# Two MLPs in a written order, with their norms turned by token halves

## The chip, the cores and the metric

One core of a Trainium2 chip runs the whole program. It has a matrix engine (TensorE, PE; its weight loads are listed apart as PEld), a vector engine (VectorE, DVE), an activation engine (ScalarE, ACT), a general engine (GpSimd, POOL) and a queue that issues the DMAs (SyncE, SP). Each works through its own list of instructions in order and waits on semaphores for the others. The metric is the time of one execution on the device in microseconds, smaller being better.

## The reference

Two residual layers over 512 tokens of 1024 features, all in fp32. Layer 0 mixes tokens by latent attention (MLA), layer 1 by an mLSTM; each mixer is followed by the same kind of MLP:

```python
def sqrelu_mlp(h, w1, w2):                       # w1 1024 x 4096, w2 4096 x 1024
    return jnp.square(jax.nn.relu(h @ w1)) @ w2

for i in range(2):                               # mixer 0: MLA, mixer 1: mLSTM
    x = x + mixer(rms_norm(x, norm_mix[i]))
    x = x + sqrelu_mlp(rms_norm(x, norm_ffn[i]), ffn_w1[i], ffn_w2[i])
```

`rms_norm` divides each token's row by the root of its mean square and multiplies by a gain per feature.

## The kernel before

The program has four stages in a row: MLA, MLP 0, mLSTM, MLP 1. x lies in SBUF with tokens on the partitions, as eight tiles `xs[t, f]` of 128 tokens by 512 features.

Every fp32 product is made of three matmuls in a rounded format: each operand is split into a high part (a cast) and a low part (operand less high part), and `mm3` (L174 to L176) adds high x high, high x low and low x high. So each weight tile of 128 x 1024 that arrives by DMA (`wr` for w1 and the mixers, `tw` for w2) costs a cast on ACT (`wh`, L160) and a subtraction on DVE (`wl`, L164).

A stage ends with `out_proj`: eight matmul groups that add to x on DVE (L700), and then the next stage's norm. The norm squares x on ACT (L251, the row sums fall out of it), turns x on PE with 128 x 128 transposes (`turn`, L238), and splits what comes out of PSUM into high (`xg`, ACT, L255) and low part (`xg`, DVE, L256), with the gain. The factor 1/rms per token is applied later: in an MLP to what is added to x, in the mixers by rows or columns. `rows_sb` (L198, L200, L232) spreads the factors along a row for mLSTM.

An MLP (`ffn`) has 32 "first" products, F0 to F31: each takes 128 of the 4096 hidden features, 8 x 3 matmuls of 512 columns (all tokens), then relu and square on ACT into `z` (L735, L737). Four of them make a chunk. The second product works by chunks of 512 hidden features. Tokens, hidden and output features are halved, and the 2 x 2 block product is made of seven products (`product`, L766) and not of eight: the price is four sums of z (L743 to L746, 256 columns each) and four sums of w2 (t1 to t4, L761 to L764, 1024 columns) on POOL. The blocks of w2 are called b11, b12, b21, b22. The seven z operands are split by a cast on ACT (`hh`, L748) and a subtraction on DVE (`hl`, L749), in pieces of 768 and 1024 columns. A product, P(c, 0) to P(c, 6), is 12 matmuls of 512 columns, and its result is added to x on DVE with the token's factor (`x<-tp,r,x`, L784).

The order: MLA is written out engine by engine, and its instructions are pinned to program order by the wrappers `ipe`, `idve`, `iact` and `ipool`. Everything after it, so `out_proj`, both MLPs and the mLSTM, is ordered by the scheduler that builds the program; the code gives it six F ahead (`lead = 6`) and one F after products 0, 2, 4 and 5 of a chunk. Each engine runs the list so made in order. PSUM banks come from the pools `mm` (three banks of 512 columns), `tp` (four) and `po` (one). At the end of MLP 0 the norm of mLSTM is turned in token halves (`Norm.half`) after the last two products; MLP 1 turns x itself (`out`, L806, L808) and stores it by DMA.

## Time and profile before

| what | value |
|---|---|
| median of 3 runs | 1155.81 us (1153.32 to 1156.1) |
| the profiled execution, its own time | 1154.43 us |
| its span | 1152.6 us |
| mean granted clock of TensorE | 0.991 |
| PE, DVE, ACT, POOL busy | 97%, 72%, 49%, 39% |

The span runs from the first to the last instruction of the profile. A row of the timeline gives the start, the busy time, engine, line, operation, output and inputs by the program's names, and in square brackets how long the engine stood idle before it and what it waited for. A matmul's busy time overlaps the next one's, so the pace of matmuls is read from their starts. The chain of work that ended last is 87% PE.

### The profile page before, as it was taken

How to read it: one execution, taken by the hardware profiler on the slowest of the kernel's cores; microseconds unless marked ns; L12 is line 12 of the kernel's file. 1: busy time of each engine (PE TensorE's matmuls, PEld its weight loads, DVE VectorE, ACT ScalarE, POOL GpSimd, SP SyncE). 2: the span in 40 equal slices, each digit the busy share in tenths (PEclk: the TensorE clock that was granted, in tenths of full speed). 3: DMA queues.
4: the chain of work that ended last, by engine and by line, in shares of the span. 5: the costliest groups of instructions: out<-in, count | busy, mean ns of one | idle time of the engine just before them, and what ended most of it. 6: DMA issues, size and time to landing. Idle time of an engine off the chain costs nothing.

```text
span 1152.6 us, 15433 instructions
## 1 busy us (share of the span) xinstructions
PE 1113.0 (97%) x5682; PEld 944.3 (82%) x5682; DVE 835.5 (72%) x1289; ACT 564.7 (49%) x962; POOL 451.8 (39%) x475
## 2 busy tenths in 40 slices
PE   7899999999999999999989999989999999999997
PEld 7889987878888888888778898877888888888875
DVE  7689997446788788778966465534477788788787
ACT  4578776455445444544454343333544454444542
POOL 6677785115355335434401011100265245335441
PEclk9999999999999999999989999999999999999999
DMA  6301111341432442343013222223422432442222
GB/s 205 109 24 47 38 56 40 126 163 57 128 109 63 122 128 80 103 129 92 19 58 109 73 74 73 79 57 103 146 76 89 129 110 63 121 127 82 66 73 74
DMA packets 31916, 104.27 MB, mean 90 GB/s; under 512 B 3424, under 2 KB 6240, under 8 KB 31840
## 3 DMA queue, kind: packets, MB, share of 16 engines
q1 hardware_dynamic: 31840, 103.27, 29.2%
q8 instruction: 45, 0.74, 0.3%
q14 instruction: 31, 0.25, 0.1%
HBM read 101.16 MB, written 2.10 MB: 90 GB/s over the span
## 4 chain that ended last, share of the span: by engine, by line
PE 87%; DVE 7%; issue 2%; POOL 2%; ACT 1%; DMA 1%; SPq 0%; DVEq 0%; ACTq 0%; POOLq 0%
PE mm L174 14%; PE mm L175 14%; PE mm L176 14%; PE tp L779 7%; PE tp L781 7%; PE tp L780 7%; PE tp L80 7%; PE mm L80 5%; PE tp L175 2%; PE tp L176 2%; PE tp L174 2%; DVE wl L164 2%; PE po L80 2%; DVE x L784 2%; PE mm L238 1%
## 5 line engine op out<-in xcount | busy, mean ns | idle before, releaser
L174 PE MATMUL mm<-xg,wh 128*128 128x512 f32 x640 | 251.2, 393 | 0.1
L176 PE MATMUL mm<-xg,wl 128*128 128x512 f32 x640 | 249.4, 390 | 0.0
L175 PE MATMUL mm<-xg,wh 128*128 128x512 f32 x640 | 249.2, 389 | 0.0
L164 DVE TENSOR_TENSOR wl<-wr,wh 128x1024 fp32r<-128x1024 f32 (+2 forms) x108 | 139.0, 1288 | 147.7 <-ACT wh L160 146.4
L160 ACT CAST wh<-wr 128x1024 fp32r<-128x1024 f32 (+2 forms) x108 | 111.1, 1029 | 252.7 <-PE mm L175 198.1
L164 DVE TENSOR_TENSOR wl<-tw,wh 128x1024 fp32r<-128x1024 f32 x112 | 185.6, 1658 | 49.6 <-ACT wh L160 49.6
L160 ACT CAST wh<-tw 128x1024 fp32r<-128x1024 f32 x112 | 117.8, 1055 | 122.2 <-PE mm L175 58.8
L780 PE MATMUL tp<-wl,hh 128*128 128x512 f32 x440 | 172.2, 391 | 2.3 <-DVE wl L164 2.3
L779 PE MATMUL tp<-wh,hh 128*128 128x512 f32 x440 | 170.5, 390 | 1.3 <-DVE x L784 1.3
L781 PE MATMUL tp<-wh,hl 128*128 128x512 f32 x440 | 171.4, 390 | 0.0
L784 DVE SCALAR_TENSOR_TENSOR x<-tp,r,x 128x512 f32<-128x512 f32 x220 | 158.9, 741 | 1.2 <-PE tp L781 1.2
L174 PEld LDWEIGHTS mm<-xg,wh 128*128 128x128 f32 x640 | 120.3, 188 | 25.9 <-issue 1.0
L175 PEld LDWEIGHTS mm<-xg,wh 128*128 128x128 f32 x640 | 120.3, 188 | 25.4 <-issue 1.0
L176 PEld LDWEIGHTS mm<-xg,wl 128*128 128x128 f32 x640 | 120.2, 188 | 24.9
L749 DVE TENSOR_TENSOR hl<-z,hh 128x768 fp32r<-128x768 f32 x64 | 105.2, 1644 | 12.1 <-ACT hh L748 12.1
L780 PEld LDWEIGHTS tp<-wl,hh 128*128 128x128 f32 x440 | 82.6, 188 | 21.5 <-DVE wl L164 4.5
L779 PEld LDWEIGHTS tp<-wh,hh 128*128 128x128 f32 x440 | 82.6, 188 | 19.0 <-ACT t L251 1.5
L781 PEld LDWEIGHTS tp<-wh,hl 128*128 128x128 f32 x440 | 82.6, 188 | 16.9
L743 POOL TENSOR_TENSOR z<-z 128x256 f32<-128x256 f32 x32 | 23.6, 737 | 175.3 <-ACT z L737 175.3
L748 ACT CAST hh<-z 128x768 fp32r<-128x768 f32 x64 | 60.5, 945 | 43.8 <-POOL z L746 42.8
L761 POOL TENSOR_TENSOR tw<-tw,tw 128x1024 f32<-128x1024 f32 x16 | 38.3, 2394 | 92.7 <-DMA tw<-in_w 90.1
L745 POOL TENSOR_TENSOR z<-z 128x256 f32<-128x256 f32 x32 | 25.5, 796 | 121.8 <-ACT z L737 121.8
(283 smaller groups left out, 2065.0 us busy)
## 6 DMA issues: line engine op xcount, KB each, us to landing
wr<-in_w SPq DMA_DIRECT2D x64, 512.0 KB, 3.6
tw<-in_w SPq DMA_DIRECT2D x64, 512.0 KB, 3.7
wr<-in_w_qkv SPq DMA_DIRECT2D x8, 640.0 KB, 3.9
wr<-in_w_oa SPq DMA_DIRECT2D x8, 512.0 KB, 3.6
wr<-in_w_mo SPq DMA_DIRECT2D x8, 512.0 KB, 3.6
wr<-in_w_ob SPq DMA_DIRECT2D x8, 512.0 KB, 3.6
wr<-in_w_v SPq DMA_DIRECT2D x6, 512.0 KB, 4.0
wr<-in_w_z SPq DMA_DIRECT2D x8, 336.0 KB, 4.4
```

The source lines that it names most:

```text
L80: return lambda *args, **kw: tc.keep_in_program_order(f(*args, **kw)) if self.on else f(*args, **kw)
L160: act.copy(hi[:, :n], raw[:, :n])
L164: dve.tensor_sub(lo[:, :n], raw[:, :n], hi[:, :n].bitcast(F32))
L174: pe.matmul(out, lhsT=lh, rhs=rh, start=start, stop=False)
L175: pe.matmul(out, lhsT=lh, rhs=rl, start=False, stop=False)
L176: pe.matmul(out, lhsT=ll, rhs=rh, start=False, stop=stop)
L748: nc.scalar.copy(hi[:, b], zp[:, b])
L749: nc.vector.tensor_sub(lo[:, b], zp[:, b], hi.bitcast(F32)[:, b])
L779: pe.matmul(ps, lhsT=lh, rhs=rh, start=new and p == 0, stop=False, skip_group_check=skip)
L780: pe.matmul(ps, lhsT=lh, rhs=rl, start=False, stop=False, skip_group_check=skip)
L781: pe.matmul(ps, lhsT=ll, rhs=rh, start=False, stop=p == 1, skip_group_check=skip)
L784: nc.vector.scalar_tensor_tensor(xs[k], ps, r2[:, k[0]:k[0] + 1], xs[k], op0=mult, op1=add)
```

## The change

1. `out_proj` is pinned to program order. Its last group of products goes by token blocks. After block 2 the first token half of the norm (`half(0, m)`, 16 transposes) is turned, then block 3's matmuls follow. The second half is left in `norm.tail`, and the MLP does it between its first products. F0's weight is split in `out_proj` already.
2. The MLP's first two products F0 and F1 are multiplied in two token halves each, 48 matmuls of 256 columns in place of 24 of 512.
3. All other work of the MLP is in a written order on PE, DVE, ACT and POOL: a list of units (F or P), weights split two units ahead and loaded four ahead, the z splits one or two units after the square, and the sums of w2 at fixed units, t2, t3 and t4 written over b11, b12 and t1.
4. The last chunk uses eight plain products of 12 matmuls, without sums.
5. At the end of MLP 0 the norm halves are turned between the last products, and features 4 to 7 of half 1 after the first V product of mLSTM. The factors are made by halves, and mLSTM's `rows_sb` moves behind the gates.
6. At the end of MLP 1 x is turned and stored between the last products, its last piece by single token blocks. Buffers for temporaries fall from 3 to 2, those for w2 grow from 5 to 6.

```diff
+    def out_proj(wsrc, lhs, layer, z0=None, w0=None):
+
+
+        z1 = [ps_tp() if z0 else ps_mm() for _ in range(3)] + [pp.tile([P, 512], F32, tag="po", bufs=1, name=nm("po"))]
+        todo = [(1, z1)]
+        if not z0:
+            z0 = [ps_tp() for _ in range(NB)]
+            todo.append((0, z0))
+        for j in range(3):
+            for f, z in todo:
+                w = load_w(wsrc[f, j], D)
+                for t in range(NB):
+                    for k in (2 * j, 2 * j + 1):
+                        o_mm(z[t], w, k, t, lhs, ipe)
+        last = [(z0, w0, (KD - 1,)) if w0 else (z0, load_w(wsrc[0, 3], D), (KD - 2, KD - 1)),
+                (z1, load_w(wsrc[1, 3], D), (KD - 2, KD - 1))]
+        norm = Norm(C_NF + layer * KD)
+        iact.on = True
+        for t in range(NB):
+            for z, w, ks in last:
+                for k in ks:
+                    o_mm(z[t], w, k, t, lhs, ipe)
+            for f, (z, _, _) in enumerate(last):
+                idve.tensor_add(xs[t, f], xs[t, f], z[t])
+            if t == 0:
+                norm.first = split_w(load_raw(a["w1"][layer, 0], D), D, iact, idve)
+            elif t == 2:
+                for m in range(0, KD, 2):
+                    norm.half(0, m)
+            for f in range(2):
                 norm.square(t, f)
-            for m in range(4 * f, 4 * f + 4):
-                norm.block(m)
-        return norms.append(norm)
+        norm.tail = [lambda m=m: norm.half(1, m, ps_tp) for m in range(0, KD, 2)]
+        iact.on = False
+        norms.append(norm)
 
     norms = []
...
+        def s_sum(c, n):
+
+            b = lambda n: tw[c, n]
+            if n == "t1":
+                tw[c, n] = fp.tile([P, D], F32, tag="tw", bufs=6, name=nm("tw"))
+                ipool.tensor_sub(b("t1"), b("b12"), b("b11"))
+            else:
+                x, y, to = {"t2": ("b22", "t1", "b11"), "t3": ("b22", "b12", "b12"), "t4": ("b21", "t2", "t1")}[n]
+                ipool.tensor_sub(b(to), b(x), b(y))
+                tw[c, n] = b(to)
...
+        def l_mm(th, f, t, part=slice(0, 12)):
+            ps = bank["L", f][t]
+            todo = []
+            for h in range(2):
+                wh, wl = ws["L", f"b{h + 1}{f + 1}"]
+                for p in range(2):
+                    lh, ll = (x[:, ((A11, A12), (3, A22))[th][h], t * P:(t + 1) * P] for x in hs[NC - 1, p])
+                    rh, rl = (x[:, p * 512:(p + 1) * 512] for x in (wh, wl))
+                    todo += [(lh, rh), (lh, rl), (ll, rh)]
+            for n in range(12)[part]:
+                ipe.matmul(ps, lhsT=todo[n][0], rhs=todo[n][1], start=n == 0, stop=n == 11)
...
+        units = [("F", i) for i in range(5)]
+        n = 5
+        for c in range(NC - 1):
+            for k in range(7):
+                units.append(("P", c, k))
+                if k in ((0, 2, 4, 5) if c < NC - 2 else (0, 1, 3)):
+                    units.append(("F", n))
+                    n += 1
+        at = {u: s_ for s_, u in enumerate(units)}
+
+        def ahead(s_):
+
+            if s_ + 4 < len(units) and units[s_ + 4][0] == "F":
+                f_load(units[s_ + 4][1])
+            if s_ + 2 < len(units):
+                u = units[s_ + 2]
+                if u[0] == "F":
+                    f_split(u[1])
+                else:
+                    s_split(u[1], u[2])
+                    if u[2] == 0:
+                        s_sum(u[1], "t2")
+                    elif u[2] == 1:
+                        s_sum(u[1], "t4")
+
+
+        ws["F", 0] = norm.first
+        f_load(1)
+        f_load(2)
+        ps = [ps_mm(), ps_mm()]
+        f_mm(ps[0], 0, HALVES[0])
+        for do in norm.tail[:2]:
+            do()
+        f_split(1)
+        f_mm(ps[1], 1, HALVES[0])
+        for do in norm.tail[2:]:
+            do()
+        u_ = norm.stat()
+        idve.reciprocal(r2, u_)
+        f_load(3)
+        f_split(2)
+        f_mm(ps[0], 0, HALVES[1])
+        f_post(ps[0], 0)
+        f_mm(ps[1], 1, HALVES[1])
+        f_load(4)
+        f_split(3)
+        f_post(ps[1], 1)
+        s_load(0, ("b11", "b12"))
+        s_sum(0, "t1")
+        s_load(0, ("b21", "b22"))
+        s_sum(0, "t3")
+        for s_ in range(2, len(units)):
+            u = units[s_]
+            if u[0] == "F":
+                ps = ps_mm()
+                f_mm(ps, u[1])
+                ws.pop(u)
+            else:
+                post = s_mm(u[1], u[2])
...
+            ahead(s_)
+            s_now[0] = s_
+            while later and later[0][0] <= s_:
+                later.pop(0)[1]()
+            if u[0] == "F":
+                f_post(ps, u[1])
+            else:
+                post()
+                c, k = u[1], u[2]
+                if k == 2:
+                    s_load(c + 1, ("b11", "b12"))
+                elif k == 4:
+                    s_load(c + 1, ("b21", "b22"))
+                elif k == 5 and c < NC - 2:
+                    s_sum(c + 1, "t1")
+                elif k == 6 and c < NC - 2:
+                    s_sum(c + 1, "t3")
+                if c == NC - 2 and k > 3:
+                    if k == 4:
+                        l_split("b11", False)
+                    elif k == 5:
+                        l_split("b21", False)
+                    else:
+                        l_split("b12", True)
         nxt = None if last else Norm(C_NM + KD)
-        lead, i = 6, 0
...
+        for n, (th, f) in enumerate(((0, 0), (0, 1), (1, 0), (1, 1))):
+            bank["L", f] = [ps_tp(), ps_tp()]
+            for t in range(2):
+                if last and n == 3 and t == 1:
+                    l_mm(th, f, t, slice(0, 8))
+                    out(4, (2,))
+                    l_mm(th, f, t, slice(8, 12))
+                else:
+                    l_mm(th, f, t)
+                if n == 0 and t == 0:
+                    l_split("b22", True)
+                if n == 2 and t == 0:
+                    half(0, (0, 2, 4, 6))
+                if n == 3 and t == 0:
+                    half(1, (0, 2))
+                y_add(2 * th + t, f, bank["L", f][t])
+                if not last:
+                    nxt.square(2 * th + t, f)
+        if last:
+            out(4, (3,))
+        else:
+            nxt.tail = [lambda m=m: nxt.half(1, m, ps_tp) for m in (4, 6)]
             norms.append(nxt)
+        iact.on = ipool.on = False
...
+                if h == 0 and t == 0:
+                    iact.on = True
+                    for do in norm.tail:
+                        do()
+                    iact.on = False
+                    roots(1)
                 nc.scalar.activation(vh[:, t, 0:DV], ps[:, 0:DV], AF.Copy, scale=r[:, t:t + 1])
```

*ACT at the start of MLP 0, before.* `wh` are weight casts (3456 and 3490 are those of F0 and F1), `t,ssq` squares of x, `xg` the norm's high parts.

```order
L160 CAST wh_3303<-wr_3301 128x1024
L160 CAST wh_3456<-wr_3454 128x1024
L160 CAST wh_3490<-wr_3488 128x1024
L255 ACTIVATE xg_3335<-mm_3360,cst 128x512
L255 ACTIVATE xg_3336<-mm_3367,cst 128x512
L251 ACTIVATE t_3388,ssq_3351<-x_3189 128x512
L251 ACTIVATE t_3390,ssq_3351<-x_3193 128x512
L251 ACTIVATE t_3392,ssq_3351<-x_3197 128x512
L160 CAST wh_3534<-wr_3532 128x1024
```

After the change, same place (3463 is F1's weight, and F0's was cast further up; `tp` banks hold half 1):

```order
L80 ACTIVATE xg_3298<-mm_3382,cst 128x256
L80 ACTIVATE t_3391,ssq_3307<-x_3183 128x512
L80 ACTIVATE t_3393,ssq_3307<-x_3185 128x512
L80 ACTIVATE t_3406,ssq_3307<-x_3187 128x512
L80 ACTIVATE t_3408,ssq_3307<-x_3189 128x512
L80 ACTIVATE xg_3291<-tp_3445,cst 128x256
L80 ACTIVATE xg_3292<-tp_3445,cst 128x256
L80 ACTIVATE xg_3293<-tp_3454,cst 128x256
L80 ACTIVATE xg_3294<-tp_3454,cst 128x256
L80 CAST wh_3463<-wr_3415 128x1024
```

F1's weight cast stood ahead of the first part of the norm, and now it stands behind four squares and four splits of half 1.

*ACT at the end of MLP 0, before.* Squares and splits of mLSTM's norm.

```order
L255 ACTIVATE xg_3434<-mm_5881,cst 128x256
L251 ACTIVATE t_5979,ssq_3450<-x_3197 128x512
L251 ACTIVATE t_5981,ssq_3450<-x_3201 128x512
L255 ACTIVATE xg_3435<-mm_5881,cst 128x256
L255 ACTIVATE xg_3436<-mm_5890,cst 128x256
L160 CAST wh_6191<-wr_6189 128x1024
L251 ACTIVATE t_5983,ssq_3450<-x_3195 128x512
L251 ACTIVATE t_5985,ssq_3450<-x_3199 128x512
L255 ACTIVATE xg_3437<-mm_5890,cst 128x256
```

After; 5998 and 6197 are weights of mLSTM (V and q), still placed by the scheduler:

```order
L80 ACTIVATE xg_5769<-mm_5867,cst 128x256
L80 ACTIVATE xg_5770<-mm_5867,cst 128x256
L80 ACTIVATE xg_5771<-mm_5876,cst 128x256
L80 ACTIVATE xg_5772<-mm_5876,cst 128x256
L80 ACTIVATE xg_5773<-mm_5885,cst 128x256
L160 CAST wh_5998<-wr_5996 128x1056
L80 ACTIVATE xg_5774<-mm_5885,cst 128x256
L160 CAST wh_6197<-wr_6195 128x1024
L80 ACTIVATE xg_5775<-mm_5894,cst 128x256
L80 ACTIVATE xg_5776<-mm_5894,cst 128x256
```

The squares of half 0 have moved ahead, and two casts of mLSTM weights stand between the splits of half 0.

*POOL at a chunk boundary in the middle of MLP 0, before.* `z` rows are the sums of z, `tw` rows t1 to t4.

```order
L761 TENSOR_TENSOR tw_4003<-tw_3996,tw_3995 128x1024
L762 TENSOR_TENSOR tw_4004<-tw_3998,tw_4003 128x1024
L743 TENSOR_TENSOR z_3877<-z_3877 128x256
L744 TENSOR_TENSOR z_3877<-z_3877 128x256
L746 TENSOR_TENSOR z_3877<-z_3877 128x256
L763 TENSOR_TENSOR tw_4005<-tw_3998,tw_3996 128x1024
L764 TENSOR_TENSOR tw_4006<-tw_3997,tw_4004 128x1024
```

After, with DVE's list of the same place behind it (3984 is the low part of b11, whose tile 3817 t2 is written over):

```order
L80 TENSOR_TENSOR z_3850<-z_3850 128x256 x4
L80 TENSOR_TENSOR tw_3956<-tw_3819,tw_3817 128x1024
L80 TENSOR_TENSOR tw_3817<-tw_3894,tw_3956 128x1024
L80 TENSOR_TENSOR tw_3819<-tw_3894,tw_3819 128x1024
L80 TENSOR_TENSOR tw_3956<-tw_3892,tw_3817 128x1024
```

```order
L80 TENSOR_TENSOR wl_3984<-tw_3817,wh_3983 128x1024
L80 TENSOR_TENSOR hl_3929<-z_3850,hh_3928 128x1024
L80 TENSOR_TENSOR wl_4007<-wr_3946,wh_4006 128x1024
L80 SCALAR_TENSOR_TENSOR x_3183<-tp_3710,r_740_3414,x_3183 128x512
L80 SCALAR_TENSOR_TENSOR x_3187<-tp_3711,r_740_3414,x_3187 128x512
L80 TENSOR_TENSOR wl_4030<-tw_3956,wh_4029 128x1024
```

The four sums of w2 stand in one block behind the sums of z, where before t1 and t2 went in among them.

## Rows read from the trace of the kernel before

**Rows 1.** the page's busy line of TensorE: busy us, share, instructions

```profile
PE 1113.0 (97%) x5682; PEld 944.3 (82%) x5682; DVE 835.5 (72%) x1289; ACT 564.7 (49%) x962; POOL 451.8 (39%) x475
```

**Rows 2.** stretches: length, PE, PEld, DVE, ACT, POOL busy, granted clock, DMA share, GB/s

```profile
248.50:268.50 20.00, 20.00 (x90) 16.55 (x89) 7.18 (x7) 8.38 (x12) 6.74 (x6) 1.00 0.42 144
586.00:591.00 5.00, 4.29 (x15) 2.77 (x14) 2.99 (x8) 3.51 (x8) 0.00 (x0) 0.58 0.01 3
804.00:812.00 8.00, 6.26 (x35) 4.91 (x34) 6.62 (x12) 6.81 (x13) 0.00 (x0) 0.79 0.51 186
```

**Rows 3.** timeline of PE, MLA to MLP 0: start, us, operation, [idle, releaser]

```profile
242.24 1.60 PE L238 MATMUL mm<-cst,x 128*128 128x128 f32 x12
245.71 2.11 PE L238 MATMUL mm<-cst,x 128*128 128x128 f32 x12 [1.88 <-DVE xg L256]
247.93 0.50 PE L174 MATMUL mm<-xg,wh 128*128 128x512 f32 x1
```

**Rows 4.** timeline of PE, mLSTM to MLP 1

```profile
804.23 1.60 PE L238 MATMUL mm<-cst,x 128*128 128x128 f32 x12
807.49 4.28 PE L238 MATMUL mm<-cst,x 128*128 128x128 f32 x20 [1.66 <-DVE xg L256]
812.15 0.40 PE L175 MATMUL mm<-xg,wh 128*128 128x512 f32 x1
```

**Rows 5.** timeline of PE, MLP 0 to mLSTM

```profile
544.55 0.39 PE L779 MATMUL tp<-wh,hh 128*128 128x512 f32 x1
585.61 2.05 PE L200 MATMUL tp<-t,ones 128*128 128x512 f32 x2 [0.61 <-ACT xg L255]
590.93 0.36 PE L174 MATMUL mm<-wh,xg 128*128 128x264 f32 x1 [0.71 <-DVE xg L256]
```

**Rows 6.** timeline of ACT, splits of norm halves, MLP 0 to mLSTM

```profile
585.04 0.84 ACT L255 ACTIVATE xg<-mm,cst 128x256 fp32r<-128x256 f32 x2 [0.37 <-PE mm L238]
586.18 0.86 ACT L255 ACTIVATE xg<-mm,cst 128x256 fp32r<-128x256 f32 x2 [0.31 <-DVE xg L256]
```

**Rows 7.** timeline of ACT and DVE, weight split and squares

```profile
242.71 1.03 ACT L160 CAST wh<-wr 128x1024 fp32r<-128x1024 f32 x1
244.22 0.62 ACT L251 ACTIVATE t<-x 128x512 f32<-128x512 f32 x1
244.74 0.19 ACT L251 ACTIVATION_READ_ACCUMULATOR t<-x 128x1 f32 x1
401.45 1.22 DVE L164 TENSOR_TENSOR wl<-wr,wh 128x1024 fp32r<-128x1024 f32 x1 [2.78 <-ACT wh L160]
```

**Rows 8.** timeline of POOL and DVE, a sum and a low part at once

```profile
435.99 2.40 POOL L761 TENSOR_TENSOR tw<-tw,tw 128x1024 f32<-128x1024 f32 x1
437.04 2.44 DVE L164 TENSOR_TENSOR wl<-tw,wh 128x1024 fp32r<-128x1024 f32 x1 [0.34 <-ACT wh L160]
```

**Rows 9.** timeline of DVE and POOL, residual adds, sums and low part of z

```profile
402.59 1.47 DVE L784 SCALAR_TENSOR_TENSOR x<-tp,r,x 128x512 f32<-128x512 f32 x2
403.98 1.05 DVE L749 TENSOR_TENSOR hl<-z,hh 128x768 fp32r<-128x768 f32 x1
402.65 0.74 POOL L743 TENSOR_TENSOR z<-z 128x256 f32<-128x256 f32 x1 [1.45 <-ACT z L737]
```

**Rows 10.** timeline of PE and DVE at the end

```profile
1142.87 0.39 PE L781 MATMUL tp<-wh,hl 128*128 128x512 f32 x1
1143.10 2.70 PE L238 MATMUL mm<-cst,x 128*128 128x128 f32 x20
1147.74 0.69 DVE L806 COPY t<-mm 128x512 f32<-128x512 f32 x1 [2.39 <-ACT t L808]
```

**Rows 11.** timeline of PE, cadence of 256 columns

```profile
639.92 0.28 PE L175 MATMUL mm<-wl,xg 128*128 128x256 f32 x1
640.04 0.28 PE L176 MATMUL mm<-wh,xg 128*128 128x256 f32 x1
```

**Rows 12.** timeline of PE, last head of mLSTM

```profile
757.04 0.44 PE L994 MATMUL tp<-cst,hb 128*128 128x128 f32 x2 [3.59 <-DVE hb L987]
```

More of the change, by code (lines that the diff above doesn't have):

```diff
@@ L673, in mla @@
                     o_unit(*ready[0])
[L674 removed]
+        for k, m in fill:
             o_unit(k, m)
         load_x()
[L677 removed]
+        out_proj(a["w_oa"], oT, 0, zo, wo[3])
     def o_mm(ps, w, k, t, lhs, pe=nc.tensor):
@@ L798, in out, with split @@
-        def out(th, m):
+            hs[c, p] = hi, lo
+            def split(b):
+                iact.copy(hi[:, b], z[:, b])
+                idve.tensor_sub(lo[:, b], z[:, b], hi.bitcast(F32)[:, b])
+            if plain:
+                later.append([s_now[0] + 1, lambda: split(slice(0, 4))])
+                return
+            ipool.tensor_add(z[:, S1], z[:, A21], z[:, A22])
+            ipool.tensor_sub(z[:, S2], z[:, S1], z[:, A11])
+            ipool.tensor_sub(z[:, S3], z[:, A11], z[:, A21])
@@ L800, in out @@
+        def out(m, ts):
             ps = ps_mm()
-            for n in range(2):
-                for t in range(2):
-                    turn(ps, (2 * n + t) * P, m + n, 2 * th + t)
+            nt = len(ts)
+            for n in range(4 // nt):
+                for i, t in enumerate(ts):
+                    turn(ps, (nt * n + i) * P, m + n, t)
             o = tmp()
-            if m % 4:
-                nc.vector.tensor_copy(o, ps)
-            else:
-                nc.scalar.copy(o, ps)
@@ L831, in ffn @@
-        if not last:
+            if m % 4 and nt > 1:
+                idve.tensor_copy(o, ps)
+            else:
+                iact.copy(o, ps)
+            nc.sync.dma_start(yT[m:m + 4 // nt, :, ts[0] * P:(ts[-1] + 1) * P].rearrange("m p t -> p m t"),
+                              o.rearrange("p (m t) -> p m t", t=nt * P))
+        units = [("F", i) for i in range(5)]
[6 more added lines that the diff above has]
+                    n += 1
@@ L1008, in trunk @@
         mlstm(pool)
-    with stage("ffnp1", 3) as pool:
+    with stage("ffnp1", 2) as pool:
         ffn(pool, 1, True)
```

229 lines of the change are left out of this document (95 added, 134 removed).

## The prediction, made before the result was known

> **What bounds the kernel now.** I read the page's busy shares first: TensorE (PE) is busy 97% of the span [rows 1], so a gain can only come from the few stretches in which it waits, or from fewer matmuls. Next the busy time by stretch: in 20 us of steady MLP work PE is busy for all 20.00 us with 90 matmuls, or 0.2267 us a piece after rounding over the whole MLP [rows 2]; both MLPs keep that pace from the first product to the 32nd "first" product. So nothing is to be had inside an MLP, and what can be had lies at five seams. Then the timeline of PE at each seam, which shows what it waited for.
>
> *MLA to MLP 0* [rows 3]: the last out_proj matmul gives way at 242.23, 24 transposes follow with an idle stretch of 1.88 us that ends on a VectorE (DVE) split of the normed input, and the first product starts at 247.93 (248.04 in effect, because its second matmul waits too). That is 5.8 us, of which the 24 transposes at 0.12 are 2.9: a loss of 2.9.
>
> *MLP 0 to mLSTM* [rows 5]: from the end of the 32nd first product (544.55) to the first V matmul (590.93, in effect 591.0) 46.5 us pass for 132 matmuls (29.9 us), 32 transposes (3.8) and two for the R row. The R row's matmuls take 2.05 us since the granted clock is 0.58 of full in that stretch [rows 2], so partly at 1.2 and partly at 2.4 GHz. Loss: some 12.
>
> *mLSTM to MLP 1* [rows 4]: 804.23 to 811.92 (the row at 812.15 less one matmul), 32 transposes of 0.12 = 3.8, loss 3.9, with a clock of 0.79 [rows 2].
>
> *The end* [rows 10]: the last matmul starts at 1142.87 and the last copy ends at 1148.43; the span ends 4.2 later. From the 32nd first product (1108.41) it is 44.2 us.
>
> *mLSTM's last head* [rows 12]: 3.59 us idle before the last transposes.
>
> **The change, part by part.** The profiled execution took 1154.43 us (span 1152.6); the median of the runs is 1155.81, so 1.4 is added at the end.
>
> *Twelve more matmuls per MLP* (the last chunk by eight plain products of 12 instead of seven): 12 x 0.2267 = 2.72 us each, on the path, charged below to the second and fourth seam.
>
> *Seams one and three.* Half 0 of the norm is now turned before the last token block of out_proj. Its four banks of 512 columns come from a pool of three, so the fourth waits until the splits of the first are through; those stand on DVE behind the two residual adds of block 2. Residual add and split end some 2.6 us after block 2's last matmul, three banks of transposes take 1.44: 1.2 lost. Then F0 is multiplied in its first half (24 matmuls at 0.12 [rows 11] = 2.9) and 8 transposes of half 1 follow. What is late next is the weight of F1. In the new order its cast on ScalarE (ACT) stands behind four squares and the four splits of half 1, and before the change it was done ahead of the norm. ACT's queue from block 2's end: the first bank through at 2.5, three more banks at 1.14 each [rows 6], 5.9; four squares at 0.81 [rows 7], 9.1; two banks of half 1, 11.2; the cast 1.03, 12.2; and DVE's low part 1.22 more [rows 7], 13.4. PE by then has 16 transposes (1.92), the wait (1.2), nine matmuls of block 3 (2.04), F0's half (2.87) and 8 transposes (0.96) = 9.0, and two matmuls of F1 (0.24) before it needs the low part: it stands for 13.4 - 9.24 = 4.2. F0 and F1 in halves cost 2 x 24 x (2 x 0.1197 - 0.2267) = 0.6. After a wait of that length the clock may be halved, as it is at seam three now after 1.66 idle: 8 us at 0.79 are 3.4 us at the low level, 1.7 lost. Seam one stays at full clock now after 1.88, so there it is a cost of 0 to 1.7, and I take it. Seam one: 1.2 + 4.2 + 0.6 + 1.7 = 7.7 against 2.9, **4.8 worse** (3.1 with the clock up). Seam three: there the accumulators lie in the same pool and the wait comes out at 4.0, 1.2 + 4.0 + 0.6 + 1.7 = 7.5 against 3.9, **3.6 worse** (1.9). If ACT's splits run at 0.42 apiece without waiting for DVE, F1's wait shrinks to 2; if the squares slip behind the residual adds it grows to 6.
>
> *Seam two.* The halves are turned between the last products. What remains is 29.9 us of matmuls, 24 transposes (2.9), 1.2 for the fourth bank as above, and a wait of half 1: ACT has two casts of mLSTM weights between the splits of half 0, and these need buffers that the third product still reads. After that product ACT and DVE have two casts (2.06), three splits (1.4), DVE's last split (0.47) and two residual adds (1.5), 5.4 in all, beside 2.72 of PE: 2.7 left over. 36.7 against 46.5 saves 9.8. Back go 2.72 (the plain products), 8 transposes after the first V product (0.96) and the R row, done later at full clock (0.9): **5.2 better**. Without the wait of half 1 it is 7.9, with a halved clock 3.5.
>
> *Seam four.* 29.9, 28 transposes between the matmuls (3.4), the last residual add (0.95), 4 transposes (0.5), a copy (0.6), a wait for a buffer of output (0.9, from the present one-for-one use of buffers) and the same 4.2 after it: 40.4 against 44.2, less 2.72, **1.1 better** (-1 to 2).
>
> *Last head of mLSTM.* Eight transposes wait for the slowest of the four normed blocks, and not two: **0.4 worse** (0 to 1).
>
> *The written order inside the MLPs.* The work is the same, but DVE's and GpSimd's (POOL's) can't be regrouped any more. Rows show what that may cost: a DVE subtraction of two tiles in SBUF that starts while POOL subtracts two tiles takes 2.44 us, twice its 1.22, and ends 1.05 us after POOL's 2.40 [rows 8]. A residual add with an input in PSUM takes its usual 0.74 beside POOL [rows 9]. The Trainium skill ("SBUF — State Buffer", the section on the shared port pair) says why: a DVE instruction with two SBUF inputs and a GpSimd instruction that reads SBUF hold one port pair in turn, each for the whole instruction. The trace agrees (2.44 for 1.22). By that rule the two engines' times add up where their order ties them together; if they merely slowed each other a little, the term below would be nil.
>
> At each chunk boundary the new order ties this chain: after an odd first product relu and square (1.5 with the hand-over), four sums of z on POOL at 0.74 (3.0), then by turns DVE's low part of a w2 block (1.22), the low part of z (1.05), POOL's sum t1 (2.40), the low part of b11 (1.22), which t2 must await because it is written over b11, the second part of z (1.22), t2 (2.40) and the low part of the next w1 block (1.22). That is 13.7, and 15.2 with the 1.5. PE needs the last of them after 60 matmuls and two more, 62 x 0.2267 = 14.05. One after the other it is 1.1 us late at each of 12 boundaries (six per MLP); where the first low part slips between POOL's sums while those wait, it isn't late. I take a quarter, 0.25 x 12 = **3 worse** (0 to 13), nearer nil since the same amount of work loses nothing now [rows 2].
>
> Sum: -4.8 - 3.6 + 5.2 + 1.1 - 0.4 - 3.0 = 5.5 us worse; 1154.4 + 5.5 + 1.4 = **1161.3**.
>
> **Rivals.**
> - *The seams close.* If F1's weight is split in time (it needs ACT's queue some 4 us shorter than I read it), seams one and three gain 1.1 and 2.1 and not lose 8.4, seam two gains 7.9, seam four 1.1, the last head -0.4: 11.8 better, 1144; with half of it, 1150. For it: the transposes have left the dead stretch. Against it: the place of that cast on ACT. It decides from the point at which F1 waits for less than 1 us: the change is faster.
> - *It cancels.* The clock stays up at seams one and three (3.4 back) and the boundaries lose nothing (3 back): 5.5 - 6.4 = -0.9, 1155. For it: 1.88 us idle leave the clock up now.
> - *The chain at the boundaries is fully serial.* 12 x 1.1 = 13 in place of 3: 1171. By the skill's rule of the port pair this is the outcome if nothing overlaps; the rows show the turn-taking itself, not its sum over this order.
>
> **How the numbers follow.** The forecast 0.45, the seams close 0.21, it cancels 0.21, serial boundaries 0.13. What three runs can tell from no change is about 0.3%, 3.5 us: 1152.3 to 1159.3. The forecast and the serial case are slower, though a part of the forecast's own spread (clock, quarter of the chain) ends inside the 3.5; the closing seams are faster but for a small part. Slower 0.51, same 0.25, faster 0.24. The range goes from the half-closed seams, 1149, to the serial boundaries, 1172; the forecast's own is 1157 to 1166.
>
> **What would show it.** In the changed profile: (1) PE idle before the first matmuls of F1 at both MLP starts, released by DVE's low part or ACT's cast, about 3 to 5 us; (2) a granted clock under 1 in the 8 us after it; (3) from F31's end to the first V matmul about 37 us; (4) small PE waits for a low part of w1 or z once per chunk, 0.2 to 1 us, with DVE subtractions over 2 us beside them; (5) 12 matmuls more per MLP; (6) about 40 us from F31 to the end. It is wrong if PE goes from F0 into F1 within a microsecond, or if waits of PE for tiles of w2 appear in mid-chunk, for which I have no term.

## The result, and the profile after

The changed kernel took 1163.63 us (median of 4 runs, 1163.01 to 1164.69) against 1155.78 before: a ratio of 1.0074, 95% interval 1.0056 to 1.0091. That is 0.7% slower, more than the noise, and 2.3 us above the forecast of 1161.3. The profiled execution of the changed kernel took 1163.95 us with a span of 1161.9, so its span is 9.3 us longer than the 1152.6 of before.

The page, TensorE's busy line (busy us, share of the span, instructions), which answers to [rows 1]:

```profile
PE 1121.3 (97%) x5802; PEld 954.0 (82%) x5802; DVE 826.9 (71%) x1284; ACT 556.4 (48%) x969; POOL 455.7 (39%) x453
```

There are 120 matmuls more: in each MLP 12 for the plain products and 48 because F0 and F1 go by halves. The share is the same 97%, so the page alone doesn't show where 9 us went. (All pinned instructions carry the wrapper's line, L80, so they are told apart by their tiles.) PE's timeline at the seams does. First MLA to MLP 0, which answers to [rows 3] (start, us, operation, in brackets idle time and releaser):

```profile
242.74 0.63 PE L80 MATMUL mm<-cst,x 128*128 128x128 f32 x4 [1.33 <-DVE xg L80]
...
248.16 1.04 PE L80 MATMUL tp<-cst,x 128*128 128x128 f32 x8
252.84 0.51 PE L80 MATMUL mm<-xg,wh 128*128 128x256 f32 x2 [3.64 <-ACT wh L80]
254.10 0.58 PE L80 MATMUL mm<-xg,wl 128*128 128x256 f32 x1 [0.75 <-DVE wl L80]
...
265.50 0.63 PE L80 MATMUL mm<-xg,wh 128*128 128x512 f32 x2
```

The first wait is the fourth bank, the other two are F1's weight: its high part, then its low part. F2 starts at 265.50. ACT's timeline for the same time shows what F1's cast stood behind, splits of half 0 (`xg<-mm`), squares (`t<-x`) and splits of half 1 (`xg<-tp`):

```profile
241.60 0.84 ACT L80 ACTIVATE xg<-mm,cst 128x256 fp32r<-128x256 f32 x2 [0.55 <-DVE xg L80]
243.02 0.84 ACT L80 ACTIVATE xg<-mm,cst 128x256 fp32r<-128x256 f32 x2 [0.58 <-DVE xg L80]
...
247.61 0.63 ACT L80 ACTIVATE t<-x 128x512 f32<-128x512 f32 x1
...
248.24 0.61 ACT L80 ACTIVATE t<-x 128x512 f32<-128x512 f32 x1
...
249.97 0.84 ACT L80 ACTIVATE xg<-tp,cst 128x256 fp32r<-128x256 f32 x2 [0.66 <-DVE xg L80]
251.38 0.47 ACT L80 ACTIVATE xg<-tp,cst 128x256 fp32r<-128x256 f32 x1 [0.58 <-DVE xg L80]
251.76 1.03 ACT L80 CAST wh<-wr 128x1024 fp32r<-128x1024 f32 x1
```

The clock afterwards (window; length, busy PE, PEld, DVE, ACT, POOL, granted clock, DMA share, GB/s): 0.69 and 0.76 of full behind the two F1 waits, so the low level of 1.2 GHz for a part of each.

```profile
252.50:258.00 5.50, 4.40 (x23) 4.19 (x24) 1.23 (x1) 0.29 (x1) 0.00 (x0) 0.69 0.49 154
818.00:825.00 7.00, 5.64 (x33) 5.43 (x34) 1.36 (x2) 0.82 (x2) 0.00 (x0) 0.76 0.34 102
```

MLP 0 to mLSTM, which answers to [rows 5]: PE's timeline from the end of F31 (555.84) to the first V matmul.

```profile
555.84 0.39 PE L80 MATMUL tp<-wh,hh 128*128 128x512 f32 x1
...
580.69 0.63 PE L80 MATMUL mm<-cst,x 128*128 128x128 f32 x4 [1.33 <-DVE xg L80]
...
588.87 0.30 PE L80 MATMUL mm<-cst,x 128*128 128x128 f32 x1 [2.08 <-DVE x L80]
589.44 0.98 PE L80 MATMUL mm<-cst,x 128*128 128x128 f32 x7 [0.27 <-DVE x L80]
...
593.01 0.28 PE L80 MATMUL mm<-wh,xg 128*128 128x264 f32 x1
```

The stretch is 37.2 us long, against 46.5. The waits of 2.08 and 0.27 us are those of half 1's transposes. DVE's timeline shows what the residual adds that end them stood behind, two low parts of mLSTM weights among the splits of half 0:

```profile
583.86 1.26 DVE L164 TENSOR_TENSOR wl<-wr,wh 128x1056 fp32r<-128x1056 f32 x1 [1.50 <-ACT wh L160]
...
585.43 1.22 DVE L164 TENSOR_TENSOR wl<-wr,wh 128x1024 fp32r<-128x1024 f32 x1
...
587.98 1.40 DVE L80 SCALAR_TENSOR_TENSOR x<-tp,r,x 128x512 f32<-128x512 f32 x2
```

mLSTM to MLP 1, which answers to [rows 4], has the same three waits as the first seam:

```profile
807.95 0.63 PE L80 MATMUL mm<-cst,x 128*128 128x128 f32 x4 [1.20 <-DVE xg L80]
...
818.60 0.51 PE L80 MATMUL mm<-xg,wh 128*128 128x256 f32 x2 [3.50 <-ACT wh L80]
819.86 0.39 PE L80 MATMUL mm<-xg,wl 128*128 128x256 f32 x1 [0.75 <-DVE wl L80]
```

A chunk boundary in MLP 0. DVE and POOL by their timelines, and PE at the first matmuls of the F behind it:

```profile
319.06 2.80 DVE L80 TENSOR_TENSOR wl<-tw,wh 128x1024 fp32r<-128x1024 f32 x1
321.79 1.21 DVE L80 TENSOR_TENSOR hl<-z,hh 128x1024 fp32r<-128x1024 f32 x1
322.92 3.42 DVE L80 TENSOR_TENSOR wl<-wr,wh 128x1024 fp32r<-128x1024 f32 x1
```

```profile
313.76 4.64 POOL L80 TENSOR_TENSOR z<-z 128x256 f32<-128x256 f32 x4 [17.11 <-ACT z L80]
318.37 2.41 POOL L80 TENSOR_TENSOR tw<-tw,tw 128x1024 f32<-128x1024 f32 x1
322.00 6.60 POOL L80 TENSOR_TENSOR tw<-tw,tw 128x1024 f32<-128x1024 f32 x2 [1.22 <-issue]
```

The DVE rows of 2.80 and 3.42 us are subtractions of 1.22 [rows 7] that each had to let one of POOL's sums by; the last ends at 326.34. On PE the F ahead of the boundary ends at 312.23, where the next product starts, and the first matmuls of the F behind the boundary stand at:

```profile
312.23 0.39 PE L80 MATMUL tp<-wh,hh 128*128 128x512 f32 x1
...
325.83 0.61 PE L80 MATMUL mm<-xg,wh 128*128 128x512 f32 x2
326.39 0.50 PE L80 MATMUL mm<-xg,wl 128*128 128x512 f32 x1
326.73 0.62 PE L80 MATMUL mm<-xg,wh 128*128 128x512 f32 x2
```

The third starts 0.56 us after the first (0.45 at the usual pace), and the next 0.34 later (0.23). So about 0.23 us are lost at each such place: six of them 41 us apart in MLP 0, and about 2 us per MLP with the first chunk's own.

The end, which answers to [rows 10]: from F31's end (1122.00) to the span's end it is 39.9 us, against 44.2.

### The profile page after: what moved, and what is told of

It is laid out like the page before. It is cut to its first block, busy times and chain, and to the rows that moved or that the text cites. A ratio compares the mean times of both kernels' runs of the same rounds, so it can differ in the third digit from the quotient of the medians.

```text
span 1161.9 us, 15626 instructions
## 1 busy us (share of the span) xinstructions
PE 1121.3 (97%) x5802; PEld 954.0 (82%) x5802; DVE 826.9 (71%) x1284; ACT 556.4 (48%) x969; POOL 455.7 (39%) x453
## 4 chain that ended last, share of the span: by engine, by line
PE 89%; DVE 4%; ACT 2%; POOL 2%; issue 1%; DMA 1%; SPq 0%; ACTq 0%; POOLq 0%; DVEq 0%
PE mm L80 38%; PE tp L80 36%; PE mm L174 4%; PE mm L176 4%; PE mm L175 3%; PE po L80 3%; DVE xg L80 1%; DVE wl L80 1%; ACT xg L80 1%; DVE x L80 1%; PE tp L176 1%; PE tp L175 1%; PE tp L174 1%; ACT t L80 1%; POOL x L80 0%
## 5 line engine op out<-in xcount | busy, mean ns | idle before, releaser
L80 PE MATMUL mm<-xg,wh 128*128 128x512 f32 (+1 forms) x1088 | 322.9, 380 | 7.4 <-ACT wh L80 7.1
L80 POOL TENSOR_TENSOR z<-z 128x256 f32<-128x256 f32 x112 | 131.4, 1193 | 344.7 <-ACT z L80 342.5
L80 PEld LDWEIGHTS mm<-xg,wh 128*128 128x128 f32 x1088 | 202.7, 191 | 46.0 <-ACT wh L80 7.6
L80 DVE TENSOR_TENSOR wl<-tw,wh 128x1024 fp32r<-128x1024 f32 x102 | 173.1, 1697 | 74.2 <-ACT wh L80 74.2
L80 PE MATMUL mm<-xg,wl 128*128 128x512 f32 (+1 forms) x544 | 207.9, 382 | 1.5 <-DVE wl L80 1.5
L80 POOL TENSOR_TENSOR tw<-tw,tw 128x1024 f32<-128x1024 f32 x56 | 158.9, 2846 | 30.4 <-issue 29.2
L80 PE MATMUL tp<-wh,hl 128*128 128x512 f32 x424 | 165.2, 390 | 0.5 <-DVE hl L80 0.5
L80 PE MATMUL tp<-wh,hh 128*128 128x512 f32 x424 | 165.4, 390 | 0.0
L80 PE MATMUL tp<-wl,hh 128*128 128x512 f32 x424 | 165.0, 389 | 0.0
L80 DVE TENSOR_TENSOR wl<-wr,wh 128x1024 fp32r<-128x1024 f32 (+1 forms) x72 | 121.3, 1685 | 49.9 <-ACT wh L80 49.9
L80 DVE SCALAR_TENSOR_TENSOR x<-tp,r,x 128x512 f32<-128x512 f32 (+1 forms) x215 | 149.5, 733 | 9.0 <-PE tp L80 8.8
L80 ACT ACTIVATE t<-mm 128x512 f32<-128x512 f32 (+3 forms) x97 | 54.3, 560 | 200.9 <-PE mm L80 191.8
L80 ACT CAST wh<-tw 128x1024 fp32r<-128x1024 f32 x102 | 106.8, 1047 | 36.7 <-PE tp L80 28.9
L80 PEld LDWEIGHTS mm<-xg,wl 128*128 128x128 f32 x544 | 103.7, 191 | 24.8 <-DVE wl L80 6.5
L164 DVE TENSOR_TENSOR wl<-wr,wh 128x1024 fp32r<-128x1024 f32 (+2 forms) x44 | 52.7, 1199 | 60.8 <-ACT wh L160 60.7
L80 PEld LDWEIGHTS tp<-wh,hl 128*128 128x128 f32 x424 | 79.6, 188 | 18.0 <-DVE hl L80 1.4
L80 ACT CAST wh<-wr 128x1024 fp32r<-128x1024 f32 (+1 forms) x74 | 78.8, 1065 | 32.1 <-PE tp L80 27.7
L80 PEld LDWEIGHTS tp<-wh,hh 128*128 128x128 f32 x424 | 79.6, 188 | 17.1 <-issue 0.8
L80 PEld LDWEIGHTS tp<-wl,hh 128*128 128x128 f32 x424 | 79.6, 188 | 16.4
L80 DVE TENSOR_TENSOR hl<-z,hh 128x1024 fp32r<-128x1024 f32 (+1 forms) x60 | 85.2, 1420 | 3.4 <-ACT hh L80 3.4
L160 ACT CAST wh<-wr 128x1024 fp32r<-128x1024 f32 (+2 forms) x44 | 43.9, 997 | 87.3 <-PE po L80 31.3
L80 ACT CAST hh<-z 128x1024 fp32r<-128x1024 f32 (+1 forms) x60 | 56.9, 949 | 57.2 <-POOL z L80 57.2
```

The lines of the kernel that those rows point to most:

```text
L80: return lambda *args, **kw: tc.keep_in_program_order(f(*args, **kw)) if self.on else f(*args, **kw)
L160: act.copy(hi[:, :n], raw[:, :n])
L164: dve.tensor_sub(lo[:, :n], raw[:, :n], hi[:, :n].bitcast(F32))
```

## The experiments

Each was timed in rounds beside the kernel before; "the changed kernel" has 1163.6 us. Theory A is that F1's weight is late because of its place in ACT's queue; B that half 1 itself holds F1.

**F1's cast ahead of half 1's splits.**

```diff
+        f_split(1)
         f_mm(ps[0], 0, HALVES[0])
         for do in norm.tail[:2]:
             do()
-        f_split(1)
```

> The changed kernel with one edit: F1's weight is cast and its low part taken after the four squares of x but ahead of the four splits of half 1, at both MLP starts. Theory A (F1 waits because its cast stands behind those squares and splits in ACT's queue): by the changed kernel's trace the cast would run from about 248.9 to 249.9 and the low part to 251.1, with PE ready at 249.2, so F1's wait falls from 4.4 us to about 1.8 at each seam, 5 us in all, and if the clock then stays up another 1 to 1.5 each: 1155 to 1159 us. Theory B (F1 is held by the splits and transposes of half 1 themselves): F1's wait stays at 3 us or more, or F0's second half waits for what F1 gains: 1162 to 1164.

Measured: 1156.12 us, ratio to before 1.0015 (1.0006 to 1.0025). F1's two waits are 0.75 and 0.76 us at the first seam and only the second one at the other. The clock, by windows as above, stays at 1.00 at the third seam and not at the first, where it is 0.89 over 245 to 260, as it was in the changed kernel over the same window:

```profile
249.09 0.50 PE L80 MATMUL mm<-xg,wh 128*128 128x256 f32 x2 [0.75 <-ACT wh L80]
250.35 0.39 PE L80 MATMUL mm<-xg,wl 128*128 128x256 f32 x1 [0.76 <-DVE wl L80]
245.00:260.00 15.00, 13.35 (x93) 12.50 (x92) 7.88 (x16) 8.99 (x21) 0.00 (x0) 0.89 0.32 106
810.00:826.00 16.00, 15.11 (x114) 14.04 (x114) 9.07 (x17) 10.94 (x24) 0.00 (x0) 1.00 0.41 132
```

A holds, within the forecast span.

**F1's cast ahead of the squares too.**

```diff
                 for m in range(0, KD, 2):
                     norm.half(0, m)
+                norm.second = split_w(load_raw(a["w1"][layer, 2], D), D, iact, idve)
...
-        ws["F", 0] = norm.first
-        f_load(1)
+        ws["F", 0], ws["F", 1] = norm.first, norm.second
```

> The changed kernel with F1's weight cast ahead of the squares of blocks 2 and 3 as well, so straight behind the splits of half 0. Theory A: F1 waits less than 0.5 us at both seams, 4.2 each less, and the clock stays up there (1 to 1.5 each); the second half of F0 may wait 0.5 to 1 for the splits of half 1, which come 1 us later: 1152 to 1155 us, so faster than the kernel before the change. Theory B: what F1 gains is lost at F0's second half, 1160 to 1164.

Measured: 1153.93 us, ratio 0.9984 (0.9971 to 0.9997). Of F1's waits nothing is left, and the clock is 1.00 over 240 to 262 and over 804 to 822. PE's timeline there now has one wait between F0's and F1's first halves, for a residual add that DVE does behind the splits:

```profile
248.36 0.27 PE L80 MATMUL tp<-cst,x 128*128 128x128 f32 x1
249.47 0.98 PE L80 MATMUL tp<-cst,x 128*128 128x128 f32 x7 [0.84 <-DVE x L80]
250.21 0.48 PE L80 MATMUL mm<-xg,wh 128*128 128x256 f32 x2
```

One weight's place in the queues of ACT and DVE was worth 9.7 us, more than the 7.9 that the change had lost. This kernel's ten runs spread from 1149.8 to 1155.8 us; the three shortest, about 1150, have a granted clock of 0.999, the others 0.993 to 0.996.

**The second z part one unit later.** Theory C is that a chain of turns between DVE and POOL at the chunk boundary is too long; D that an order can't shorten it.

```diff
-            later.append([s_now[0] + 2, lambda: split(slice(3, 7))])
+            later.append([s_now[0] + 3, lambda: split(slice(3, 7))])
```

> The changed kernel with the second part of each z split one unit later, so that on DVE the low part of the next w1 block comes before it. Theory C (at each chunk boundary F's low part is late by 0.23 us because the z part and POOL's t2 hold the shared port one after the other ahead of it): t2 can start when b11's low part is done, F's low part follows it 1.2 us earlier than now, and the 12 gaps of 0.23 us between the first matmuls of that F vanish: 3 us less, 1160 to 1161.5 us. Theory D (the chain is as long whatever the order, since t2 only moves): the gaps stay or move to the product that uses the second z part: 1163 to 1166.

Measured: 1173.65 us, ratio 1.0167 (1.015 to 1.0184): my expectation was wrong, and by more than D allowed. DVE's timeline shows it: F's low part now comes in time, and the z part takes the next turn behind a POOL sum. What comes after it is late.

```profile
324.53 2.66 DVE L80 TENSOR_TENSOR wl<-wr,wh 128x1024 fp32r<-128x1024 f32 x1 [0.97 <-ACT wh L80]
327.11 3.43 DVE L80 TENSOR_TENSOR hl<-z,hh 128x1024 fp32r<-128x1024 f32 x1
```

PE waits for low parts of w2 in the grouped waits (waiting operation, releaser, us, times, longest), a row that the changed kernel has not:

```profile
PE tp L80 <- DVE wl L80: 5.6, 10, 0.6
```

**t1 one first product earlier.** If the chain can't be reordered, something has to leave it.

```diff
                 elif k == 4:
+                    if c < NC - 2:
+                        s_sum(c + 1, "t1")
                     s_load(c + 1, ("b21", "b22"))
-                elif k == 5 and c < NC - 2:
-                    s_sum(c + 1, "t1")
```

> The changed kernel with POOL's sum t1 of the next chunk one first product earlier, so ahead of the four z sums, in a stretch where POOL and DVE both stand idle (POOL for 17 us, DVE for 4.8). Theory C, mended (the chain at a chunk boundary is too long because each DVE low part in it pays for one POOL sum; to shorten it a sum must leave it): t1's 2.4 us leave the chain and the gaps of 0.23 and 0.1 us at 12 boundaries vanish, 3 to 4 us less: 1159.5 to 1161 us. Theory D (only the order of the waits changes; with t1's buffer taken earlier the load of b22 comes later and t2 with it): the gaps stay or grow, 1163 to 1168.

Measured: 1161.25 us, ratio 1.0056 (1.0039 to 1.0072), 2.4 less than the changed kernel. That interval overlaps the changed kernel's (1.0056 to 1.0091), so the time alone doesn't show the gain; the trace does, and the same edit shows it again under "Together". The gaps at the boundaries are gone but for the first chunk's. The two low parts at the boundary by DVE's timeline, to be held against 2.80 and 3.42:

```profile
319.05 1.21 DVE L80 TENSOR_TENSOR wl<-tw,wh 128x1024 fp32r<-128x1024 f32 x1
...
322.81 1.92 DVE L80 TENSOR_TENSOR wl<-wr,wh 128x1024 fp32r<-128x1024 f32 x1 [1.43 <-ACT wh L80]
```

C in its mended form holds, with somewhat less than forecast: without t1 in the chain the gaps are gone.

**V's weights in order at the end of MLP 0.** Theory E is that two casts of mLSTM weights between the splits hold DVE, and so the residual adds that half 1 waits for.

```diff
                     nxt.square(2 * th + t, f)
+                if not last and t == 1 and n in (1, 2):
+                    nv = 4 * (DV + 2 * MH)
+                    nxt.v.append(split_w(load_raw(a["w_v0"][n - 1], nv), nv, iact, idve))
...
+                if h == 0:
+                    iact.on = True
+                    w = split_w(load_raw(wsrc, D), D, iact, idve)
+                    iact.on = False
```

> The changed kernel with the two V weights of mLSTM's first head pinned: the first is cast before the splits of half 0 at the end of MLP 0, the second after them and after the residual adds, and the first q weight in program order too. Theory E (the 2.1 and 0.3 us waits of half 1's transposes come from the two mLSTM casts between the splits of half 0, which wait for buffers that the third product reads, and hold DVE's splits and so the residual adds behind them): the wait falls to under 0.5, 2 us less: 1161 to 1162 us. Theory F (the residual adds are late for other reasons, or the V product then waits as long for its second weight): 1163 to 1165.

Measured: 1171.12 us, ratio 1.0151 (1.0136 to 1.0167). The wait of half 1 did vanish: PE's first V matmul stands at 590.80 here, straight behind the last product. But the q weight, pinned where the program names it, came after the gates, which its product used to cover. PE's timeline behind the V products:

```profile
607.30 0.61 PE L1014 MATMUL tp<-g_lf,cst 128*128 128x16 f32 x2 [3.67 <-DVE g_lf L1010]
...
620.01 0.50 PE L174 MATMUL mm<-xg,wh 128*128 128x512 f32 x1 [1.62 <-ACT wh L80]
```

In between the clock is 0.76 (606 to 620). A second try casts q straight behind the second V weight.

```diff
+                    if n == 2:
+                        nxt.q = split_w(load_raw(a["w_mq"][0], D), D, iact, idve)
```

> The changed kernel with the two V weights pinned as in the run before, and the first q weight cast straight behind the second V weight. Theory E: the waits of 2.1 and 0.3 us before half 1's transposes vanish, and, with the q weight in time, nothing is lost after the V products: 1161 to 1162 us. Theory F: what is gained there is lost behind the V products again (the gates or the q product wait): 1163 or more.

Measured: 1162.54 us, ratio 1.0069 (1.0054 to 1.0084), only 1.1 better, which is not clear of the noise. Half 1's wait is gone again, and 0.56 and 0.33 us came back as waits for residual adds, now behind two low parts on DVE, before the transposes that follow the first V product (594.61 and 595.26). E holds for the wait; of its 2.3 us, 0.9 came back at once as other waits.

**The last chunk by seven again.** With `PLAST` in the order A11, S1, S2, A12, S4, S3, A22 and half 0 turned between the last products:

```diff
-        for c in range(NC - 1):
+        for c in range(NC):
...
+                turned = {(NC - 1, 5): (0, (0, 2)), (NC - 1, 6): (1, (4, 6))}.get(u[1:])
```

> The changed kernel with the last chunk by seven products again (12 matmuls fewer per MLP, with its sums of z and w2), in the written order, half 0 turned after the sixth product's first token block and the rest of half 1 after the first V product. Theory G (the twelve matmuls cost what they last, and the sums hide as in the other chunks): 2 x 2.72 us less, 1158 to 1159 us. Theory H (with no first products left between them, the sums on POOL and the low parts on DVE hold each other up, and PE waits as long as the matmuls lasted): 1162 to 1168.

Measured: 1175.11 us, ratio 1.0178 (1.0163 to 1.0194). 24 matmuls fewer, and 11.5 us more than the changed kernel: theory H, and stronger than I had it. DVE's low parts take up to 2.79 us among POOL's sums there, the residual adds queue behind them, and the products, which need the banks these adds empty, wait. PE's timeline at the end of MLP 0:

```profile
567.92 0.47 PE L80 MATMUL tp<-wh,hh 128*128 128x512 f32 x1 [2.16 <-DVE x L80]
...
591.92 0.72 PE L80 MATMUL mm<-cst,x 128*128 128x128 f32 x4 [3.45 <-DVE xg L80]
594.00 0.77 PE L80 MATMUL tp<-wh,hh 128*128 128x512 f32 x1 [1.36 <-DVE x L80]
```

In the grouped waits PE, writing to `tp` banks, waits 9.1 us for residual adds, nine times, a row that the changed kernel has not. That is theory H, but not all of the 11.5 us: POOL's last sum ends at 576.3, and the wait of 3.45 us comes later, when DVE does two low parts of V weights and the splits of the norm; the clock over 584 to 600 is 0.79. At the end of MLP 1, which splits no norm, the gaps between the starts of the products' matmuls add up to about 4.9 us, against the 2.7 saved. How the rest divides between the sums and this order of turning is not shown. So in this written order the eight plain products are worth their 5.4 us of matmuls. Whether another order of the seven would do better was not tried.

**The fourth bank behind block 3**, on top of F1's early cast:

```diff
-                for m in range(0, KD, 2):
+                for m in range(0, KD - 2, 2):
                     norm.half(0, m)
...
+            elif t == 3:
+                norm.half(0, KD - 2)
+                norm.second = split_w(load_raw(a["w1"][layer, 2], D), D, iact, idve)
```

The edit moves a second thing: F1's split now stands behind the squares of block 2 too.

> The kernel with F1's cast ahead of the squares (1153.9 us), and in addition the fourth bank of half 0 turned after block 3's matmuls. If the 1.3 us wait of the fourth bank at both seams is a matter of the three banks alone, it vanishes, and with it the 0.8 us wait of half 1's first transposes, whose residual adds then stand ahead of the last splits: 2.6 to 4 us less, 1150 to 1151.5 us. If F0 then waits for its last two feature blocks instead: 1153 to 1155.

Measured: 1152.71 us, ratio 0.9987 (0.9978 to 0.9996). The waits of 1.33 and 0.84 us at the first seam are gone but for 0.22, and at the third PE has none left. But F0 now waits for its last two feature blocks, whose splits stand behind block 2's squares: twice at the end of its first half two matmuls take 0.75 us where 0.24 is usual, and each pair starts 0.28 us after the matmul before it where 0.12 is usual.

```profile
246.72 0.91 PE L80 MATMUL mm<-xg,wh 128*128 128x256 f32 x2
...
247.75 0.91 PE L80 MATMUL mm<-xg,wh 128*128 128x256 f32 x2
```

From half 0's transposes to the second halves of F0 and F1 it is 13.36 us at the first seam against 13.80 with the early cast alone, and 13.35 against 13.72 at the third: 0.8 us gained in all. By the ratios (0.9987 and 0.9984) the time is the same. So the alternative named last in the expectation (1153 to 1155 us) describes what came about better than the first, though the time lies just under its range.

**Half 1 before F0.** The same kernel, without what the halves are for:

```diff
-        f_mm(ps[0], 0, HALVES[0])
-        for do in norm.tail[:2]:
+        for do in norm.tail:
             do()
...
+        f_mm(ps[0], 0)
+        f_split(2)
+        f_post(ps[0], 0)
+        f_mm(ps[1], 1)
```

> The kernel with F1's cast early and the fourth bank behind block 3 (1152.7 us), but with all of half 1 turned before F0, and F0 and F1 whole (48 matmuls of 512 columns and not 96 of 256). Theory I (leaving half 1 for later is what hides it): after block 3 PE has only transposes to do until ACT has two squares and the first splits behind it, a wait of 2 to 4 us at each MLP start less the 0.6 that whole products save, and a lower clock now and then: 1156 to 1161 us. Theory J (with the cast in time, the halves bring nothing): 1151 to 1153.5.

Measured: 1158.28 us, ratio 1.003 (1.0019 to 1.0041), 5.6 worse than with the halves. PE's timeline at the first seam:

```profile
246.30 2.29 PE L80 MATMUL tp<-cst,x 128*128 128x128 f32 x15 [2.06 <-DVE x L80]
250.33 1.42 PE L80 MATMUL mm<-xg,wh 128*128 128x512 f32 x2 [1.74 <-ACT xg L80]
```

At the third seam the waits are 1.20 and 2.17 us. The clock is 0.84 over 240 to 262 and 0.93 over 800 to 825, where the kernel with the halves has 1.00, so a part of the 5.6 us is the clock behind these waits. Theory I: once the weight is in time, turning by halves pays for itself.

**Together.** t1 earlier, F1's early cast and the late fourth bank in one kernel:

> The kernel with F1's cast early and the fourth bank behind block 3 (1152.7 us), with t1 one first product earlier. If the two effects are independent the 2.4 us of t1 come off: 1150 to 1151 us.

Measured: 1150.59 us, ratio 0.9956 (0.994 to 0.9971): 2.1 less than the kernel with the late fourth bank, and the two intervals don't touch. Then with the V weights as in the first of the two tries, and q's cast behind the splits after the first V product:

```diff
                         do()
+                    norm.q = split_w(load_raw(a["w_mq"][0], D), D, iact, idve)
                     iact.on = False
```

> The kernel of the run before (t1 earlier), with the two V weights pinned round half 0's splits, and the first q weight cast behind the splits that are left for after the first V product. Theory E: the 2.1 us wait of half 1's transposes at the end of MLP 0 goes, the 0.9 us that the earlier variant lost behind the first V product is not lost, and the q product doesn't wait: 2 us off, 1148 to 1149 us. If q's cast comes too late there, PE waits at the gates again: 1151 or more.

Measured: **1146.36 us, ratio 0.9923 (0.9907 to 0.9938)**, the best here: 8.6 us under the kernel before, 17 under the changed one. It is 4.2 under the run before by medians, where 2 was forecast, and 2.8 by the two profiled executions (1148.72 and 1145.96); what makes up the excess is not shown. At the end of MLP 0 PE has one wait left, by its timeline:

```profile
573.19 0.63 PE L80 MATMUL mm<-cst,x 128*128 128x128 f32 x4 [1.40 <-DVE xg L80]
```

At last that one was taken on, by the fourth bank of half 0 one token block later at the ends of both MLPs:

```diff
-                    half(0, (0, 2, 4, 6))
+                    half(0, (0, 2, 4))
+                if n == 2 and t == 1:
+                    half(0, (6,))
```

> The kernel of the run before, with the fourth bank of half 0 at the end of both MLPs turned one token block of matmuls later. The 1.3 us wait of that bank at the end of MLP 0 goes: 1 us off. At the end of MLP 1, where x is copied and not split, little changes. 1147 to 1148.5 us.

Measured: 1146.76 us, ratio 0.9927 (0.9909 to 0.9946), the same. PE's timeline shows why (its execution is the longest of the four, 1148.93 us): the wait of 1.40 went, and half 1's transposes wait again for residual adds, which stand behind the fourth bank's splits on DVE.

```profile
580.96 0.98 PE L80 MATMUL mm<-cst,x 128*128 128x128 f32 x7 [2.08 <-DVE x L80]
```

## Why the prediction was right, step by step

The changed kernel's span is 9.3 us longer, by landmarks in the two traces that have the same work behind them:

| stretch | predicted, us | measured, us |
|---|---|---|
| before the first seam (MLA, not changed) | 0 | +0.7 |
| first seam, to F2 | +4.8 | +5.9 |
| MLP 0, F2 to F31: 12 matmuls and the chain | +2.7 +1.5 | +2.7 +2.0 |
| second seam, F31's end to V; then behind V | -9.8; +1.9 | -9.3; +1.8 |
| last head and third seam, to F2 | +0.4 +3.6 | +0.1 +4.8 |
| MLP 1, F2 to F31 | +2.7 +1.5 | +2.7 +2.2 |
| fourth seam, F31's end to the span's end | -3.8 | -4.3 |
| sum | +5.5 | +9.3 |

The 2.7 us of the plain products are booked here where they run, in the MLPs. The forecast missed the span by 3.8 us and the medians only by 2.3: it had added 1.4 us because the profiled execution of before lay that far under its median, while that of the changed kernel lies 0.3 above. So a part of the closeness is luck.

*First and third seam.* The mechanism held in each part: the fourth bank 1.2 forecast and 1.33 and 1.20 measured; F1's wait 4.2 and 4.0 forecast, 4.4 and 4.25 measured. The size of F1's wait is right partly because two errors cancel: a bank of splits took ACT 1.42 us (241.60 to 243.02), not 1.14, with 0.55 to 0.58 of it spent waiting for DVE, and a square took 0.63 (247.61 to 248.24), not 0.81, because the busy times that I added up overlap. The clock was a choice between 0 and 1.7 us per seam; 0.69 over 5.5 us and 0.76 over 7 us make 1.7 at both. The early cast showed the cause and not only the place. What was undersized is the sum: about 1 us per seam, of which some 0.8 are short waits round the second halves of F0 and F1, for which I had no term (at the first seam starts at 261.49 and 261.78 where 0.12 is usual, then 0.74 for two matmuls that usually take 0.24).

*Second seam.* 36.7 forecast, 37.2 measured. The wait of half 1 came out at 2.08 and 0.27 against 2.7, for the reason given; two runs with the V weights pinned took it away.

*Written order inside the MLPs.* 3 us forecast, 4.2 measured. The chain is where I put it, ending at the low part of the w1 block behind the boundary, but it doesn't behave as I wrote. I added up 15.2 us, 1.1 more than PE's 14.05, and took a quarter because the first low part might slip between POOL's sums at some boundaries. The trace has 14.1 us (312.23 to 326.34), one link after the other. It is shorter because the links are: POOL's four z sums with two DVE low parts among them took 4.6 us (313.76 to 318.4) and not 5.3, and DVE rows of 1.21 us follow each other at 1.13. So it is late by a little at every boundary, 0.23 us on PE, and not by 1.1 at some. That my quarter came to 0.25 us a boundary is luck; the rival of the serial chain had the shape and not the size. The first chunk's own wait had no term. The subtractions of 1.22 us that take 2.80 and 3.42 beside POOL's sums show the two engines taking turns. The trace so agrees with the Trainium skill ("SBUF — State Buffer", section "Who interferes with whom"), which says that a DVE instruction with two SBUF inputs contends with a GpSimd instruction that reads SBUF. My forecast for reordering it (the z part later) was wrong: I moved one link and not the number of turns.

*Fourth seam.* 40.4 forecast, 39.9 measured.

Three slips in the working change little: two banks of splits at 1.14 make 2.3 and not 2.1, a quarter of 12 times 1.1 is 3.3 and not 3, and by [rows 8] the subtraction ends 1.09 us after POOL's sum and not 1.05.

*The rival that failed by one line.* "The seams close" decides, I wrote, from the point at which F1 waits less than 1 us, with 1144 if everything closes. With F1's cast early the kernel was 0.16% faster than before, and with t1, the V weights and the fourth bank moved as well 1146.4. So the change's loss came from the place of one weight's split: with it mended the rest of the change is worth next to nothing, and two more edits, t1 and the V weights, make it gain.

What stays open: the 0.7 us before the first seam lies in unchanged work. In the thirteen profiles that share this work (the changed kernel and the twelve variants) half 0's transposes start at 239.1 to 240.7 us, so 0.7 is inside the scatter; a wait at the very start of the program, 5.1 to 6.0 us in these profiles, varies too. Why the combined kernel gained more than forecast, and how the loss of the seven products divides, is open as well.

## What to carry to other kernels

When transposes or splits are deferred into the next stage, look at what now stands behind them in the splitting engine's queue: the next weight's cast must be ahead of the deferred work. Two engines that take turns were not helped here by another order of the same turns; what helped was to take one operation out of the tight stretch, into one where both stand idle. A written order gives the waits to whoever writes it: each fix here uncovered the next wait on the same engine, so read the whole queue behind an instruction before moving it.
